# Gates of a linear recurrence: each head on its own 64 rows, both gates in one tile, the two heads in turn into two banks

## The chip, the core and the metric

The kernel runs on one core of one Trainium2 chip. The time is that of one execution on the device, in microseconds (us). The engines of the core are TensorE (matmuls; PE in the rows, PEld for its weight loads), VectorE (DVE), ScalarE (ACT), GpSimd (POOL) and SyncE (SP), which issues the DMAs. TensorE writes to PSUM, a memory of eight banks, from where VectorE or ScalarE fetch its results.

## The reference, cut to what matters

One layer of a hybrid recurrent decoder, on 1024 prompt tokens and 8 x 4 sample tokens (1056 columns in the kernel). A projection of x feeds a gated linear recurrence (RG-LRU) and a diagonal state-space branch (S5); their merge goes through an output projection, a layer norm, a convolutional feed-forward part (up, convolution, gelu, down) and a second layer norm. The change is in the gates of the recurrence:

```python
xh = xf.reshape(B_, L, LRU_HEADS, LRU_HEAD_DIM)          # 16 heads of 64
r = sigmoid(einsum('blhi,hij->blhj', xh, w_a).reshape(B_, L, D_LRU) + b_a)
i = sigmoid(einsum('blhi,hij->blhj', xh, w_x).reshape(B_, L, D_LRU) + b_x)
log_a = LRU_C * r * log_sigmoid(lam)
a = exp(log_a)
bterm = sqrt(max(-expm1(2 * log_a), 0)) * (i * xf)
h = scan(a, bterm)                                        # h_t = a_t h_{t-1} + b_t
```

Each head multiplies its 64 channels by a 64 x 64 matrix, once for gate r (`w_a`) and once for gate i (`w_x`).

## The kernel before

Activations lie with channels on the 128 partitions and tokens along the columns. The 1024 recurrence channels are eight groups j = 0 to 7 of 128, each a pair of heads ("head pair j"). All large products are made with three matmuls instead of one: an operand is split into a rounded part (`...h`, type fp32r, by ScalarE's copy) and the rest (`...l`, by VectorE's subtraction), and h x h, l x h and h x l add up in a bank (`mm3`, `split`).

For each j: `lru_in` makes the projection `psx` (three chunks of 352 columns, 24 matmuls each), copies it out and convolves it to `xc`; `lru_gate` and `s5_gate` make the projections `psl` and `psg` for the merge; `lru_rec` splits `xc` into `xch` and `xcl`, makes the gates, and runs the recurrence (`av`, `bv`, `th` with VectorE's scan, `gg`). The gate weights come from the host as 128 x 256: for each gate a 128 x 128 block with the two heads' matrices on the diagonal and zeros elsewhere (`layouts`, L1715 to L1719). `lru_weights` loads and splits them. For each gate and each of three chunks of 360 columns (the padded sequence has 1080), three matmuls write one bank (`psr`), and one activation of 128 x 360 on ScalarE applies bias and sigmoid into `gt`.

The state-space branch runs in four units (0 to 3). In each, `s5_consts` makes its tables (`tmc`, `CA`, `bk`, `psk`, `BA`, `pst`, `F32t`, `BT`) and `s5_batch` its work: `psv` (plain fp32, 64 columns of weights into 64 partitions of a bank, the two halves of the partitions in turn; one fp32 matmul is two records in the trace), the copy `V`, the scans `G`, and `psy` (plain fp32, full array). `z_split` splits its result. Small products (`psr`, `psk`, `pst`, `psv`, `psy`) share two banks ("aux"); the others use six ("mm").

At the start, x arrives in slices `xr` and is split into `xh`, `xl`; the first two weight tiles (`wx` into `wh`, `wl`) arrive in pieces, and `u_tile` multiplies slice by slice (`psu`). Behind the recurrence follow the merge (`psab`, with the tile `mm`), the output projection (`pso`), and the feed-forward products (`ps`, `pd`).

The order of all instructions on every engine is set before the launch. `Program.add` records each operation with its engine, an estimated duration and its dependences; `Program.schedule` replays them and takes, among the operations that are ready, the one of the smallest number. The numbers follow the code, shifted by the entries of the table `BOOST` (`boosted("rg3")` shifts all within). Each engine then runs its list strictly in order. The durations in `schedule` are the planner's own, not the chip's.

## Time and profile before

| | us |
|---|---|
| three runs, median | 1349.86 |
| three runs, lowest and highest | 1348.16, 1350.09 |
| the profiled execution, its own time | 1348.73 |
| its span, first to last instruction | 1347.0 |
| TensorE busy in the span | 1325.2 |
| VectorE busy | 1084.9 |
| ScalarE busy | 606.1 |
| GpSimd busy | 77.7 |

Matmuls are pipelined: each has a recorded duration of about two spacings of starts, so busy times of TensorE overlap, and what a matmul costs is read from when the next one starts. "Idle before" names what the engine waited for, put down to what came last. The granted clock of TensorE is 1.00 at its upper level and 0.50 at its lower one.

### The profile page before, as it was taken

The numbers are of one execution on the slowest core, as the hardware profiler recorded it, in microseconds if no ns is written. First come the engines' busy times: TensorE is split into PE (matmuls) and PEld (weight loads), VectorE is DVE, ScalarE is ACT, GpSimd is POOL, SyncE is SP. The second block draws the span as 40 slices with busy tenths as digits, with TensorE's granted clock in tenths as the row PEclk, the third lists the DMA queues.
The fourth block names the chain that finished last, engine by engine and source line by source line (L and its number), as shares of the span: only waits on it lengthen the run. The fifth ranks groups of instructions, "written<-read, shape, count | busy, mean of one in ns | idle before, by whom it ended". The sixth has DMA issues, their size and how long they took to land.

```text
span 1347.0 us, 24659 instructions
## 1 busy us (share of the span) xinstructions
PE 1325.2 (98%) x10044; PEld 1316.4 (98%) x10044; DVE 1084.9 (81%) x1823; ACT 606.1 (45%) x802; POOL 77.7 (6%) x184
## 2 busy tenths in 40 slices
PE   8999999999999999999999999999999999999996
PEld 8999999999999999999999999999999999999996
DVE  6996868697979986879998878878878884555797
ACT  6335545558678433355333333333332453433463
POOL 0000101110301100000100000000000000000000
PEclk9999999999999999999999999999999999999998
DMA  7524141437878770042343323232222497855251
GB/s 277 137 62 105 56 113 64 120 122 231 295 245 297 275 253 33 33 142 93 107 153 115 105 107 105 96 112 89 102 89 89 142 361 286 304 181 164 66 207 65
DMA packets 89330, 201.88 MB, mean 150 GB/s; under 512 B 11008, under 2 KB 40960, under 8 KB 89216
## 3 DMA queue, kind: packets, MB, share of 16 engines
q1 hardware_dynamic: 89216, 200.30, 44.4%
q8 instruction: 79, 1.29, 0.4%
q14 instruction: 35, 0.29, 0.1%
HBM read 142.17 MB, written 58.09 MB: 149 GB/s over the span
## 4 chain that ended last, share of the span: by engine, by line
PE 88%; DVE 7%; ACT 1%; DMA 1%; issue 1%; SPq 0%; DVEq 0%; ACTq 0%
PE ps L397 37%; PE pd L397 18%; PE pso L397 7%; PE psab L397 7%; PE psg L397 6%; PE psx L397 4%; PE psl L397 4%; PE psr L397 2%; PE psu L397 1%; PE psy L397 1%; DVE tmp L329 1%; DVE xc L341 1%; DVE tmc L329 1%; DVE wl L329 1%; DVE zl L329 1%
## 5 line engine op out<-in xcount | busy, mean ns | idle before, releaser
L397 PE MATMUL pd<-fh,dh 128*128 128x264 f32 x672 | 192.3, 286 | 0.0
L397 PE MATMUL pd<-fh,dl 128*128 128x264 f32 x672 | 191.0, 284 | 0.0
L397 PE MATMUL pd<-fl,dh 128*128 128x264 f32 x672 | 191.0, 284 | 0.0
L397 PEld LDWEIGHTS pd<-fh,dh 128*128 128x128 f32 x672 | 126.5, 188 | 0.2
L397 PEld LDWEIGHTS pd<-fl,dh 128*128 128x128 f32 x672 | 126.3, 188 | 0.2
L397 PEld LDWEIGHTS pd<-fh,dl 128*128 128x128 f32 x672 | 126.5, 188 | 0.0
L329 DVE TENSOR_TENSOR dl<-dx,dh 128x1024 fp32r<-128x1024 f32 x48 | 58.2, 1220 | 46.8 <-ACT dh L366 46.8
L397 PE MATMUL pso<-mm,wh 128*128 128x264 f32 x512 | 95.5, 287 | 0.0
L366 ACT CAST dh<-dx 128x1024 fp32r<-128x1024 f32 x48 | 49.2, 1048 | 83.3 <-PE pd L397 74.6
L341 DVE SCALAR_TENSOR_TENSOR ac<-fx,con,ac 128x1072 f32<-128x1072 f32 x48 | 64.0, 1334 | 28.0 <-ACT ac L362 27.4
L366 ACT CAST wsh<-wa 128x1024 fp32r<-128x1024 f32 x24 | 25.3, 1052 | 135.1 <-DVE wa L329 126.6
L397 PEld LDWEIGHTS pso<-mm,wh 128*128 128x128 f32 x512 | 79.8, 188 | 0.5
L397 PE MATMUL pso<-mm,wl 128*128 128x264 f32 x256 | 72.7, 284 | 0.0
L329 DVE TENSOR_TENSOR wl<-wx,wh 128x1024 fp32r<-128x1024 f32 (+2 forms) x48 | 54.1, 1130 | 18.4 <-PE psx L397 8.0
L362 ACT ACT_TABLE_LOAD x52 | 66.7, 1283 | 2.0 <-PE psy L397 1.1
L366 ACT CAST wh<-wx 128x1024 fp32r<-128x1024 f32 (+2 forms) x48 | 47.0, 982 | 39.3 <-DMA wx<-wall 19.3
L397 PE MATMUL psab<-zh,wh 128*128 128x352 f32 (+1 forms) x200 | 63.6, 318 | 0.0
L397 PE MATMUL psab<-zl,wh 128*128 128x352 f32 (+1 forms) x200 | 63.6, 318 | 0.0
L397 PE MATMUL psab<-zh,wl 128*128 128x352 f32 (+1 forms) x200 | 63.4, 317 | 0.0
L366 ACT CAST fh<-fr 128x1056 fp32r<-128x1056 f32 x42 | 44.6, 1074 | 41.0 <-PE pd L397 25.7
L397 PE MATMUL psg<-xh,wh 128*128 128x352 f32 x192 | 62.6, 326 | 0.0
L397 PE MATMUL psl<-xh,wh 128*128 128x352 f32 x192 | 62.6, 326 | 0.0
(346 smaller groups left out, 4593.9 us busy)
## 6 DMA issues: line engine op xcount, KB each, us to landing
f<-gt SPq DMA_DIRECT2D x84, 264.0 KB, 2.1
wx<-wall SPq DMA_DIRECT2D x42, 512.0 KB, 4.6
fr<-f SPq DMA_DIRECT2D x30, 528.0 KB, 4.8
wa<-wall SPq DMA_DIRECT2D x29, 512.0 KB, 4.4
wg<-wall SPq DMA_DIRECT2D x24, 512.0 KB, 3.6
dx<-wall SPq DMA_DIRECT2D x24, 512.0 KB, 4.6
dx<-s SPq DMA_DIRECT2D x24, 512.0 KB, 5.8
fr<-f SPq DMA_DIRECT2D x24, 264.0 KB, 3.6
```

What stands on the lines that cost most here:

```text
L329: pr.add("DVE", 69 + 1.0417 * fsize(out), lambda: V.tensor_tensor(out=out, in0=a, in1=b, op=op), [a, b], [out])
L341: lambda: V.scalar_tensor_tensor(out=out, in0=a, scalar=sc, in1=b, op0=op0, op1=op1),
L362: pr.add("ACT", c, lambda: S.activation(out=out, in_=a, func=f, bias=bias, scale=scale), [a] + [x for x in (bias, scale) if isap(x)], [out ...
L366: pr.add("ACT", (51 if psum(a) else 93) + 0.8333 * fsize(out), lambda: S.copy(out, a), [a], [out])
L397: T.matmul(o, lhsT=l, rhs=r, start=st, stop=sp, skip_group_check=skip)
```

## The change

The gate weights become one 128 x 128 tile per head pair: the rows of a head hold its two 64 x 64 matrices side by side, for the second head in swapped order. `lru_rec` issues, per chunk of columns, six matmuls of 64 rows x 128 columns of weights on 360 columns: the three of the first head (rows 0 to 63) into one aux bank and the three of the second (rows 64 to 127) into the other, in turn. Each bank then holds both gates of one head. Four activations of 64 partitions take them out, two per bank; one of the two writes to the other half of the partitions than it reads, and `bx` is rolled by 64 on the host for it. The planner's estimate for such a group is `share` and `more` in `mms`. The table `BOOST` is replaced as a whole (a line of each stands below), so that every list of instructions is another one.

```diff
 BOOST = {
-    "b0": -10, "b1": 1493, "b2": 1614, "b3": 1297, "c0": 190, "c1": -1072, "c2": 199, "c3": 2328, "cb1": 225,
...
+    "b1": 820, "b2": -87, "b3": 393, "c2": -694, "c3": 168, "cb0": -165, "cb1": 153, "cb2": 474, "cb3": -4263,
...
-    def mms(calls, skip=False):
+    def mms(calls, skip=False, share=1.0, more=0.0):
...
-        pr.add("PE", cost, fn, rd, wr, lat=100.0)
+        pr.add("PE", cost * share + more, fn, rd, wr, lat=100.0)
...
         def lru_weights(j):
             with boosted(f"wg{j}"):
-                wgx = mid([2, P], name=f"wgx{j}")
-                dma(wgx[:, :, :], ins["wgate"][j])
-                wgh, wgl = mid([2, P], F32R, name=f"wgh{j}"), mid([2, P], F32R, name=f"wgl{j}")
-                split(wgx[:, :, :], wgh[:, :, :], wgl[:, :, :])
+                wgx = mid([P], name=f"wgx{j}")
+                dma(wgx[:, :], ins["wgate"][j])
+                wgh, wgl = mid([P], F32R, name=f"wgh{j}"), mid([P], F32R, name=f"wgl{j}")
+                split(wgx[:, :], wgh[:, :], wgl[:, :])
...
-                for q, bn in ((0, "ba"), (1, "bx")):
-                    gt = slot([LL], name=f"gt{j}_{q}")
-                    for c in range(NCH):
-                        n = slice(360 * c, 360 * c + 360)
-                        psg = aux([360], f"psr{j}_{q}_{c}")
-                        mms(mm3(psg[:, :], wgh[:, q, :], wgl[:, q, :], xch[:, n], xcl[:, n], True, True))
-                        with boosted("e"), boosted("erec"):
-                            act(gt[:, n], psg[:, :], AF.Sigmoid, bias=cv(bn)[:, j:j + 1])
-                    gate.append(gt)
+                gate = [slot([LL], name=f"gt{j}_{q}") for q in range(2)]
+                hf = slice(0, 64), slice(64, P)
+                for c in range(NCH):
+                    n = slice(360 * c, 360 * c + 360)
+                    pa = [aux([360], f"psr{j}_{c}_{hd}") for hd in range(2)]
+                    m = [mm3(pa[hd][:, :], wgh[hf[hd], :], wgl[hf[hd], :], xch[hf[hd], n], xcl[hf[hd], n], True, True)
+                         for hd in range(2)]
+                    mms([x for y in zip(*m) for x in y], share=0.53, more=210.0)
+                    with boosted("e"), boosted("erec"):
+                        for hd in range(2):
+                            s, o = hf[hd], hf[1 - hd]
+                            act(gate[0][s, n], pa[hd][s, :], AF.Sigmoid, bias=cv("ba")[s, j:j + 1])
+                            act(gate[1][s, n], pa[hd][o, :], AF.Sigmoid, bias=cv("bx")[o, j:j + 1])
...
-    wgate = np.zeros((NK, 2, 64, 2, 2, 64), np.float32)
+    wgate = np.zeros((NK, 2, 64, 2, 64), np.float32)
...
-            wgate[:, hd, :, q, hd, :] = a[:, hd]
+            wgate[:, hd, :, q ^ hd, :] = a[:, hd]
```

Three places in the lists of instructions. A row names the line of the code, the operation, the tile that it writes and those that it reads (with a running number of the buffer) and its shape. First TensorE at the gates of head pair 0, first chunk, before (`psr_0_0` is gate and chunk):

```order
L397 MATMUL psg_2_204<-xh_101,wl_192 128x352
L397 MATMUL psr_0_0_248<-xch_245,wgh_182 128x360
L397 MATMUL psr_0_0_248<-xcl_246,wgh_182 128x360
L397 MATMUL psr_0_0_248<-xch_245,wgl_183 128x360
L397 MATMUL psr_0_1_249<-xch_245,wgh_182 128x360
L397 MATMUL psr_0_1_249<-xcl_246,wgh_182 128x360
L397 MATMUL psr_0_1_249<-xch_245,wgl_183 128x360
L397 MATMUL psx_0_261<-xh_80,wh_199 128x352
```

The same place after (`psr_0_1` is chunk and head):

```order
L397 MATMUL psg_2_204<-xh_101,wl_192 128x352
L397 MATMUL psr_0_0_249<-xch_245,wgh_182 128x360
L397 MATMUL psr_0_1_250<-xch_245,wgh_182 128x360
L397 MATMUL psr_0_0_249<-xcl_246,wgh_182 128x360
L397 MATMUL psr_0_1_250<-xcl_246,wgh_182 128x360
L397 MATMUL psr_0_0_249<-xch_245,wgl_183 128x360
L397 MATMUL psr_0_1_250<-xch_245,wgl_183 128x360
L397 MATMUL psx_0_261<-xh_80,wh_199 128x352
```

Six matmuls stay six, and the bank changes with every one instead of every third; 24 groups of six stand in the list after, and between any two of them stand twelve or more matmuls of other tiles. In unit 3 of the state-space branch, the list before has `psv` for three of its four groups in a row; after, two, then 24 `psl` matmuls, then two.

Second, VectorE up to `xcl_512`, the split for the gates of head pair 5, before (`th_473` is the scan of head pair 4, `xc_534` the convolution of head pair 7):

```order
L354 SCALAR_TENSOR_TENSOR th_473<-av_471,bv_472 128x1080
L329 TENSOR_TENSOR gg_401<-gg_401,th_473 128x1024
L329 TENSOR_TENSOR zl_507<-z_505,zh_506 128x8x128
L329 TENSOR_TENSOR zl_507<-z_505,zh_506 128x4x8
L329 TENSOR_TENSOR gg_401<-gg_401,th_473 128x32
L329 TENSOR_TENSOR wl_567<-wx_565,wh_566 128x1024
L329 TENSOR_TENSOR spv_1201<-spv_1201,spz_1200 128x1024
L341 SCALAR_TENSOR_TENSOR xc_534<-xp_533,con,xc_534 128x1080
L329 TENSOR_TENSOR zl_510<-z_508,zh_509 128x8x128
L341 SCALAR_TENSOR_TENSOR xc_534<-xp_533,con,xc_534 128x1080
L329 TENSOR_TENSOR zl_510<-z_508,zh_509 128x4x8
L329 TENSOR_TENSOR xcl_512<-xc_446,xch_511 128x1080
```

The same place after:

```order
L329 TENSOR_TENSOR spv_1201<-spv_1201,spz_1200 128x1024
L329 TENSOR_TENSOR bv_472<-bv_472,gt_1_464 128x1080
L329 TENSOR_TENSOR zl_507<-z_505,zh_506 128x8x128
L329 TENSOR_TENSOR zl_507<-z_505,zh_506 128x4x8
L329 TENSOR_TENSOR av_471<-av_471,th_473 128x1080
L329 TENSOR_TENSOR wl_567<-wx_565,wh_566 128x1024
L329 TENSOR_TENSOR zl_510<-z_508,zh_509 128x8x128
L329 TENSOR_TENSOR zl_510<-z_508,zh_509 128x4x8
L348 MEMSET av_471 128x8
L341 SCALAR_TENSOR_TENSOR xc_534<-xp_533,con,xc_534 128x1080
L329 TENSOR_TENSOR xcl_512<-xc_446,xch_511 128x1080
L354 SCALAR_TENSOR_TENSOR th_473<-av_471,bv_472 128x1080
```

The scan, both products with it and one of the steps of `xc_534` now stand behind `xcl_512`; otherwise the same work stands ahead of it.

Third, SyncE's DMAs at the very start, before (`wx_73` and `wx_76` are the first two weight tiles, `xr` the slices of x, `con` the constants):

```order
L376 DMA wx_73<-wall 128x256
L376 DMA xr_79<-xT 128x352 x3
L376 DMA xr_82<-xT 128x352 x3
L376 DMA wx_73<-wall 128x256
L376 DMA wx_76<-wall 128x256
L376 DMA xr_85<-xT 128x1056
L376 DMA xr_88<-xT 128x1056
```

The same place after:

```order
L376 DMA wx_73<-wall 128x512
L376 DMA wx_73<-wall 128x256
L376 DMA xr_79<-xT 128x352 x3
L376 DMA xr_82<-xT 128x352 x3
L376 DMA con<-con 128x964
L376 DMA wx_76<-wall 128x256 x2
L376 DMA wgx_181<-wgate 128x128
L376 DMA xr_85<-xT 128x1056
```

The last 512 columns of the first weight tile moved to the front, and the constants and a gate tile ahead of the third slice of x (`xr_85`). On TensorE, `psu` follows the slices in turn in both.

## Rows read from the trace of the kernel before

**Rows 1.** The page, engines: busy us (share of the span) and instructions.

```profile
PE 1325.2 (98%) x10044; PEld 1316.4 (98%) x10044; DVE 1084.9 (81%) x1823; ACT 606.1 (45%) x802; POOL 77.7 (6%) x184
```

**Rows 2.** Waits of TensorE: us in total, times, longest us.

```profile
PE psu L397 <- ACT xh L366: 4.3, 1, 4.3
PE psr L397 <- DVE xcl L329: 2.4, 1, 2.4
PE psv L397 <- ACT V L366: 1.1, 1, 1.1
PE psk L397 <- DVE bk L345: 1.1, 1, 1.1
PE pst L401 <- DVE F32t L329: 0.6, 1, 0.6
...
```

**Rows 3.** Tile `psr`: duration min/median/max in ns, first and last start, form.

```profile
L397 PEld LDWEIGHTS psr<-xch,wgh x48: 186/188/330, 125.7 to 429.7; 128*128 128x128 f32 x48
L397 PE MATMUL psr<-xch,wgh x48: 322/327/502, 125.9 to 429.8; 128*128 128x360 f32 x48
...
L362 ACT ACTIVATE gt<-psr,con x48: 550/561/573, 126.6 to 432.4; 128x360 f32<-128x360 f32 x48
```

**Rows 4.** Tile `psv`, its weight loads, columns as in rows 3.

```profile
L397 PEld LDWEIGHTS psv<-U,BT x128: 132/137/138, 81.5 to 283.7; 128*64 128x64 f32 x128
```

**Rows 5.** Timeline of TensorE at a group of gates: start us, us, instruction.

```profile
125.87 0.33 PE L397 MATMUL psr<-xch,wgh 128*128 128x360 f32 x1
...
126.87 0.32 PE L397 MATMUL psx<-xh,wh 128*128 128x352 f32 x1
```

**Rows 6.** Timeline of TensorE around `psv` and behind `psy`.

```profile
140.24 0.32 PE L397 MATMUL psx<-xh,wl 128*128 128x352 f32 x1
140.49 1.15 PE L397 MATMUL psv<-U,BT 128*64 128x136 f32 x16
141.57 0.43 PE L397 MATMUL psl<-xh,wh 128*128 128x352 f32 x1
141.84 0.32 PE L397 MATMUL psl<-xl,wh 128*128 128x352 f32 x1
...
283.43 0.68 PE L397 MATMUL psv<-U,BT 128*64 128x136 f32 x8
...
306.12 0.42 PE L397 MATMUL psx<-xh,wh 128*128 128x352 f32 x1
```

**Rows 7.** Chain that ended last, a piece with `psy`: start us, us, what.

```profile
303.59 2.78 PE psy L397 x24
```

**Rows 8.** Timeline of TensorE at the gates of head pair 5.

```profile
374.77 0.33 PE L397 MATMUL psr<-xch,wgh 128*128 128x360 f32 x1
377.50 0.67 PE L397 MATMUL psr<-xcl,wgh 128*128 128x360 f32 x1 [2.40 <-DVE xcl L329]
...
380.63 0.34 PE L397 MATMUL psg<-xh,wl 128*128 128x352 f32 x1
```

**Rows 9.** Windows: us, busy us of PE, PEld, DVE, ACT, POOL; PEclk, DMA share, GB/s.

```profile
377.20:380.60 3.40, 3.10 (x10) 3.10 (x11) 3.40 (x4) 2.15 (x5) 0.00 (x0) 0.50 0.56 183
...
404.00:438.00 34.00, 34.00 (x212) 34.00 (x211) 33.84 (x39) 28.85 (x38) 5.76 (x4) 1.00 0.85 296
```

**Rows 10.** Timeline of VectorE ahead of that `xcl`.

```profile
363.11 2.41 DVE L354 TENSOR_TENSOR_SCAN th<-av,bv 128x1080 f32<-128x1080 f32 x1
365.55 1.23 DVE L329 TENSOR_TENSOR gg<-gg,th 128x1024 f32<-128x1024 f32 x1
...
374.78 1.34 DVE L341 SCALAR_TENSOR_TENSOR xc<-xp,con,xc 128x1080 f32<-128x1080 f32 x1
...
376.16 1.28 DVE L329 TENSOR_TENSOR xcl<-xc,xch 128x1080 fp32r<-128x1080 f32 x1
```

**Rows 11.** Timeline of TensorE, the first matmul.

```profile
4.26 0.66 PE L397 MATMUL psu<-xh,wh 128*128 128x352 f32 x1 [4.26 <-ACT xh L366]
```

**Rows 12.** DMA view of the first 40 us: GB/s in 40 slices of 1 us.

```profile
GB/s 0 13 285 279 251 278 304 295 323 285 347 370 427 420 398 422 399 392 396 398 395 409 396 393 293 220 298 103 12 0 0 82 291 152 236 292 304 211 231 386
```

More of the change, by code (lines that the diff above doesn't have):

```diff
@@ L1019, in lru_rec @@
             wgh, wgl = GW.pop(j)
-            gate = []
             with boosted(f"rg{j}"):
@@ L1697, in layouts @@
     con = np.concatenate([
-        col(i["lru_conv_w"][0].reshape(-1)), col(i["lru_conv_b"][0]), col(i["lru_ba"][0]), col(i["lru_bx"][0]),
+        col(i["lru_conv_w"][0].reshape(-1)), col(i["lru_conv_b"][0]), col(i["lru_ba"][0]), np.roll(col(i["lru_bx"][0]), 64, 0),
         col(i["lru_lambda"][0]), col(i["ln1_g"][0]), col(i["ln1_b"][0]), col(i["ln2_g"][0]), col(i["ln2_b"][0]),
@@ L1718, in layouts @@
         for hd in range(2):
-            wgate[:, hd, :, q, hd, :] = a[:, hd]
-    r = {"xT": xT, "wall": wall, "con": con, "scon": scon, "wgate": wgate.reshape(NK, P, 2, P)}
+            wgate[:, hd, :, q ^ hd, :] = a[:, hd]
+    r = {"xT": xT, "wall": wall, "con": con, "scon": scon, "wgate": wgate.reshape(NK, P, P)}
     return {k: np.ascontiguousarray(a) for k, a in r.items()}
```

68 rows, old and new, of the table BOOST are left out of this document.

## The prediction

> **What bounds the kernel now.** I read the engine line of the page first: TensorE is busy for 1325.2 of 1347.0 us, VectorE for 81%, ScalarE for 45% [rows 1]. So the change is worth what it takes from TensorE's own work, plus what it removes or adds of the moments in which TensorE stands. The second view is the list of what TensorE waited for, and it is short: 4.3 us for the first operand, 2.4 us for `xcl`, 1.1 us each for a copy of `V` and for `bk`, 0.6 us for `F32t`, and a smaller one [rows 2]. All of these lie ahead of 380 us; behind that point reordering has nothing to win.
>
> **The gates.** Before, one chunk of one gate is three matmuls of 128 rows on 360 columns, and there are 144 of them [rows 3]. They are pipelined, so their recorded 0.33 us is no price; the spacing of starts is. Six of them start at 125.87 us and the next other matmul at 126.87 us [rows 5]: 1.00 us for six, 0.166 us each, and 24 x 1.00 = 24.0 us in all.
>
> After, the count stays at 144, but each reads 64 rows, and two in a row use different halves of the array and different banks. If a pair runs together, a chunk costs three spacings instead of six. No instruction of before uses half of the rows, but `psv` uses half of the columns, in the same alternation, and is the nearest row. Sixteen `psv` take 1.15 us and eight take 0.68 us [rows 6]: eight more cost 0.47 us, 0.059 us each. `psy`, of the same 136 columns and type on the full array, takes 2.78 us for 24, 0.116 us each [rows 7]. So two halves do run together there, at the price of one.
>
> The same stretch prices the change of shape. From the last full matmul ahead of the sixteen (start 140.24 us) to the second one behind them (141.84 us) pass 1.60 us [rows 6]. Two full spacings of 0.16 and eight pairs of 0.116 make 1.25 us; 0.35 us are lost, in a gap ahead of the first `psv` and in a slow first matmul behind (0.43 us). A 64-column load took 0.137 us [rows 4] and a 128-column one 0.188 us [rows 3], and the new groups load 128 columns, so I add 0.05: 0.40 us per group. The order shows 24 groups with full-array work between all of them, so all 24 pay.
>
> A group after: 3 x 0.165 + 0.40 = 0.895 us against 1.00. **24 x 0.105 = 2.5 us gained.** The bounds: a switch that costs nothing would give 12.1 us; halves that don't run together would cost 24 x 0.40 = 9.6 us. I take 2.5, since `psv` is the one row with a partial array and both its parts are measured there.
>
> The Trainium skill, page "TensorE: Matmul & The Clock Gate", section "LDWEIGHTS (loading the stationary operand)", says that a load takes as long as its columns make it, whatever the number of rows: 107 ns for 128 columns. If the two loads of a pair also followed each other, a pair would take 0.213 us by this figure, and the gates would cost an estimated 0.9 us more than before. The page "TensorEngine Tiling (Array Packing)", section "Tiling Modes", says on the other side that different tiles load and multiply in parallel; `psv` agrees with that one for halves of the columns, and no run here shows it for halves of the rows.
>
> **The eviction.** A chunk of both gates was emptied by two activations of 128 x 360, 0.56 us each [rows 3]; now it is four of 64 x 360. Half the partitions leave the columns as they were, so I price each at the same 0.56: 48 more, 27 us on an engine that is 45% busy. Both auxiliary banks stay taken for some 2.2 us instead of 1.1, and most groups have 24 matmuls of 0.16 us (3.9 us) between them, which covers it. Between the second and third chunk of head pair 6 there are only twelve (1.9 us): I add **0.4 us** for that. The gate weights halve; their DMAs and splits lie on queues and engines with room, priced at zero.
>
> **The stall at 374.8 us.** The first matmul of the gates of head pair 5 starts at 374.77 us, the second at 377.50, because `xcl` came late [rows 8]; the granted clock is 0.50 from 377.2 to 380.6 us, the lower of its two levels, after TensorE had stood for 2.40 us [rows 8, 9]. The price: 2.73 - 0.17 = 2.56 us of standing, then 3.13 us for the ten matmuls from 377.50 to 380.63 us, which take 1.63 us at the upper level, so 1.50 more. Together 4.1 us. VectorE was busy all the way ahead of that `xcl`. In its new order the scan (2.41), its product (1.23) and one step of the next convolution (1.34) stand behind `xcl` instead of ahead of it [rows 10]: 5.0 us, twice what the standing needs. What is late next there is the last split of `z`, which still precedes `xcl`, and ScalarE's `xch`. **I take the whole 4.1 us as gained**; the other bound is zero.
>
> **The `V` wait.** In unit 3 of the state-space branch three groups of `psv` stood in a row on two banks, and the third waited 1.1 us for ScalarE [rows 2]. Now two stand in a row, then 24 full matmuls, then two, as in units 1 and 2, for which no such wait is listed. **1.1 us gained.**
>
> **The start.** The new DMA order puts 256 KB of the first weight tile ahead of everything, and the 482 KB of constants ahead of the second tile's weights. At the 280 GB/s of the first microseconds [rows 12] the first matmul, at 4.26 us before [rows 11], comes 0.9 us later, and the third slice of x, with 802 KB more ahead of it, 2.9 us later. TensorE's first pass needs these slices in turn, so it falls 2.9 us behind. Part is absorbed: the waits for `bk` and `F32t`, 1.7 us [rows 2], are set by VectorE's chain of parameters, whose inputs have the same bytes ahead of them as before. I take 2.9 - 1.7 = **1.2 us lost**; the bounds are 0 and 2.9.
>
> **The rest of the order.** From 404 to 438 us VectorE is busy for 33.84 of 34.00 us beside a full TensorE [rows 9]. An earlier TensorE finds the same backlog there. I price it at zero, because nothing on TensorE waited there, and keep it as a rival.
>
> **The sum.** -2.5 - 4.1 - 1.1 + 1.2 + 0.4 = -6.1 us. The profiled execution took 1348.73 us, so 1342.6; the median of the three runs is 1.1 us above that execution, so I forecast 1343.8 us (rounded from 1343.7).
>
> **The rivals.**
> 1. *The halves don't run together*, since halves of the rows differ from halves of the columns: both write all 128 partitions, though to two banks. For it: no row of before shows it done. Against it: `psv`. The term of -2.5 becomes +9.6: 1355.9 us, slower. It decides from the point at which a pair takes over 0.25 us: a group then costs 1.15 us, and 24 x 0.15 eats the 3.6 us that the other terms give.
> 2. *The loads of a pair follow each other.* By the load rows, 64 more columns take 0.051 us longer, so 128 columns stream in 0.102 us; a pair then takes 0.204 us, a group 1.01, in all 2.8 us more than forecast: 1346.6 us. `psv` doesn't exclude it: two loads of 64 columns would need 0.102 us, and a pair there takes 0.118.
> 3. *The switch is cheaper*, because part of the 0.35 us behind `psv` belongs to a change of type (the first matmul behind `psy`, with no change of shape, is slow too, 0.42 us [rows 6]), and the gates have the type of their neighbours. At 0.20 us per group 4.8 us less: 1339.0 us.
> 4. *The stall stays or moves* to another late operand of VectorE: 1347.9 us.
> 5. *VectorE or ScalarE takes it back* from 404 us on: VectorE is full there, and ScalarE's 28.85 of 34 us [rows 9] grow by twelve activations, 6.7 us, to over 35. TensorE then waits for banks or for its operands until most of the 6.1 us is gone: 1348.8 us.
>
> **How the numbers follow.** The forecast gets 0.42, rival 1 0.07, rival 2 0.08, rival 3 0.15, rival 4 0.13, rival 5 0.10, and 0.05 are left for waits at places that I did not follow. The time is the forecast's. The range takes in rival 3 and a little below it, and reaches up past rivals 4 and 5; it leaves out rival 1 and the cheapest switch: 1337 to 1350.5 us. A measurement can tell about 0.2%, 2.7 us, so faster means below 1347.2 us. The forecast and rival 3 lie there, most of rival 2 and a third of rivals 4 and 5: 0.74. Within 0.2% lie the rest of those: 0.17. Slower: rival 1 and part of the unknown, 0.09.
>
> **What would show it.** In the profile after: starts of a `psr` pair some 0.01 us apart and pairs 0.165 us apart (0.20 for rival 2, equal steps of 0.165 for rival 1); 0.90 + 0.32 us from the last full matmul ahead of a group to the second behind it; no wait of TensorE for `xcl` and `V`, and no second stretch at the lower clock; the first matmul near 5.2 us and a shorter wait for `bk`. I am wrong on the order if TensorE waits for VectorE or ScalarE anew, above all behind 404 us.

## The result, and the profile after

The changed kernel is slower: a median of 1357.9 us (four runs, 1355.9 to 1358.5) against 1349.0 us for the kernel before on the same chip, a ratio of 1.0064 with an interval of 1.0047 to 1.0082. The forecast was 1343.8 us and a range that ended at 1350.5. The profiled execution took 1357.9 us, with a span of 1356.1.

The engine line of the page of after, to set beside [rows 1]:

```profile
PE 1325.7 (98%) x10044; PEld 1305.4 (96%) x10044; DVE 1084.2 (80%) x1823; ACT 626.5 (46%) x845; POOL 87.9 (6%) x184
```

It tells little: TensorE is busy for as long as before in a span that is 9 us longer, so it stands for 30.4 us instead of 21.8. Where, the line doesn't say. ScalarE has 20 us more. The waits of TensorE of after (us in total, times, longest), beside [rows 2], tell more:

```profile
PE psr L397 <- ACT gt L362: 5.6, 1, 5.6
PE psu L397 <- ACT xh L366: 5.4, 1, 5.4
PE psg L397 <- ACT xp L366: 3.5, 1, 3.5
PE pst L401 <- DVE BA L329: 1.5, 1, 1.5
PE psy L397 <- POOL H L369: 1.2, 2, 1.0
PE psk L397 <- DVE bk L345: 1.0, 1, 1.0
...
```

The two waits that the prediction wanted gone, `xcl` and `V`, are gone. Two longer ones stand in their place, 5.6 and 3.5 us, on operands that it did not name, and the first operand comes 1.1 us later.

Tile `psr` of after (duration min/median/max in ns, first and last start), beside [rows 3], and TensorE's timeline at a group of gates, beside [rows 5]:

```profile
L362 ACT ACTIVATE gt<-psr,con x96: 540/557/562, 129.3 to 444.2; 64x360 f32<-64x360 f32 x96
L397 PEld LDWEIGHTS psr<-xch,wgh x48: 182/183/283, 128.5 to 441.7; 64*128 64x128 f32 x48
...
```

```profile
...
128.29 0.32 PE L397 MATMUL psg<-xh,wl 128*128 128x352 f32 x1
128.55 0.43 PE L397 MATMUL psr<-xch,wgh 64*128 64x360 f32 x2
128.82 0.33 PE L397 MATMUL psr<-xcl,wgh 64*128 64x360 f32 x2
128.99 0.32 PE L397 MATMUL psr<-xch,wgl 64*128 64x360 f32 x2
129.24 0.43 PE L397 MATMUL psx<-xh,wh 128*128 128x352 f32 x1
129.51 0.33 PE L397 MATMUL psx<-xl,wh 128*128 128x352 f32 x1
```

Each line "x2" is a pair; its two starts lie 3 ns apart, and so do the starts of its two loads. From the last full matmul ahead to the second behind pass 129.51 - 128.29 = 1.22 us (1.214 by the unrounded starts), of which 0.32 are the full ones: 0.894 us for a group.

**Where the time went.** Start of the same matmul in both traces, us:

| matmul | before | after | lag |
|---|---|---|---|
| first `psu` | 4.26 | 5.38 | +1.12 |
| last `psu` | 53.35 | 55.76 | +2.41 |
| last `psl` of head pair 0 | 81.25 | 84.56 | +3.31 |
| first `psk` of unit 3 | 247.52 | 251.16 | +3.63 |
| last `psl` of head pair 5 | 283.18 | 284.80 | +1.62 |
| last `psl` of head pair 7 | 363.03 | 364.45 | +1.41 |
| first `psab` | 393.39 | 403.98 | +10.60 |
| first `pso` | 492.49 | 502.42 | +9.93 |
| first `plsq`, near the end | 1333.66 | 1342.90 | +9.24 |

At the last `psl` of head pair 5 the lists differ: after, two groups of `psv` are still to come there, before only one. Behind the last `psv` the lag is 2.08 us.

Nearly all of the loss falls between 364 and 404 us, behind which a little is gained back. TensorE's timeline there has two holes:

```profile
364.45 0.32 PE L397 MATMUL psl<-xh,wl 128*128 128x352 f32 x1
368.24 0.43 PE L397 MATMUL psg<-xh,wh 128*128 128x352 f32 x1 [3.47 <-ACT xp L366]
...
386.23 0.32 PE L397 MATMUL psg<-xh,wl 128*128 128x352 f32 x1
392.12 1.24 PE L397 MATMUL psr<-xch,wgh 64*128 64x360 f32 x2 [5.57 <-ACT gt L362]
```

3.79 and 5.89 us from start to start, and behind each the granted clock falls, as in [rows 9]. Windows of after (busy us of PE, PEld, DVE, ACT, POOL; PEclk, DMA share, GB/s):

```profile
364.40:368.30 3.90, 0.43 (x4) 0.14 (x2) 3.59 (x4) 2.64 (x5) 0.54 (x2) 1.00 0.82 196
368.30:373.10 4.80, 4.80 (x20) 4.80 (x21) 4.80 (x4) 2.81 (x5) 4.75 (x4) 0.64 1.03 419
386.20:392.10 5.90, 0.35 (x3) 0.06 (x1) 5.87 (x7) 0.57 (x2) 5.27 (x2) 0.84 0.45 181
392.10:397.00 4.90, 4.88 (x17) 4.19 (x18) 0.45 (x1) 4.80 (x9) 0.00 (x0) 0.50 0.28 110
```

The 20 matmuls of the second window take 3.2 us at the upper level, so 1.6 are lost; the last window's 4.9 us would be some 2.5 us, by the group at 128.55 and ten spacings of 0.16. The two holes cost 3.6 + 1.6 and 5.7 + 2.4, together 13.3 us; the stall on `xcl` (4.1 us) is saved against it. 13.3 - 4.1 = 9.2, which is the step from +1.41 to +10.60.

What filled the holes stands on ScalarE and GpSimd (timelines of after):

```profile
363.38 2.21 ACT L366 CAST zh<-z 128x1024 fp32r<-128x1024 f32 x2
...
367.74 1.23 ACT L366 COPY xp<-psx 128x352 f32<-128x352 f32 x4 [1.26 <-DVE zl L329]
...
391.51 1.14 ACT L362 ACTIVATE gt<-psr,con 64x360 f32<-64x360 f32 x2 [6.09 <-POOL states L369]
```

```profile
384.22 7.25 POOL L369 COPY states<-th 128x1 f32<-128x1 f32 x2 [10.94 <-DVE th L354]
```

*First hole.* `xp` empties the banks of `psx` for the next product. It stands behind casts of `z` in ScalarE's list, and then waits another 1.26 us for VectorE's `zl`: `xp` and `z` take their buffers from the same pool (`temp`), and `zl` is the last reader of a `z`. *Second hole.* The second gate's tile takes the slot (a buffer of a pool that many tiles share) of an older `th`, two of whose last readers are copies on GpSimd of 128x1 and 128x8. They start behind the scan of `th`, which the new order puts behind `xcl`, and take 7.25 us. ScalarE waits for the slot, both auxiliary banks stay full, and TensorE waits for a bank. Before, the second gate's tile was wanted three chunks later.

### The profile page after: what moved, and what is told of

Its sections match the earlier page's. It is cut to its first block, busy times and chain, and to the rows that moved or that the text cites. A ratio compares the mean times of both kernels' runs of the same rounds, so it can differ in the third digit from the quotient of the medians.

```text
span 1356.1 us, 24760 instructions
## 1 busy us (share of the span) xinstructions
PE 1325.7 (98%) x10044; PEld 1305.4 (96%) x10044; DVE 1084.2 (80%) x1823; ACT 626.5 (46%) x845; POOL 87.9 (6%) x184
## 4 chain that ended last, share of the span: by engine, by line
PE 87%; DVE 7%; ACT 3%; issue 1%; DMA 1%; POOL 1%; SPq 0%; DVEq 0%; ACTq 0%; POOLq 0%
PE ps L397 36%; PE pd L397 18%; PE psab L397 7%; PE pso L397 7%; PE psg L397 5%; PE psx L397 5%; PE psl L397 4%; PE psr L397 1%; PE psu L397 1%; PE psy L397 1%; DMA xr<-xT 1%; DVE tmp L329 1%; DVE xc L341 1%; DVE tm L329 1%; ACT gt L362 1%
## 5 line engine op out<-in xcount | busy, mean ns | idle before, releaser
L397 PE MATMUL psg<-xl,wh 128*128 128x352 f32 x192 | 63.1, 329 | 0.0
L397 PE MATMUL psx<-xh,wh 128*128 128x352 f32 x192 | 63.1, 329 | 0.0
L397 PE MATMUL psg<-xh,wl 128*128 128x352 f32 x192 | 63.1, 328 | 0.0
```

The lines of the kernel that those rows point to most:

```text
L397: T.matmul(o, lhsT=l, rhs=r, start=st, stop=sp, skip_group_check=skip)
```

## The experiments

Ratios are against the kernel before on the same chip, with their 95% interval.

**1. The table and the gates apart.** Two kernels cross the parts of the change: the new gates with the old table, the old gates with the new table. The same table doesn't give the same lists, since the planner replays other operations with it.

```diff
 BOOST = {
-    "b1": 820, "b2": -87, "b3": 393, "c2": -694, "c3": 168, "cb0": -165, "cb1": 153, "cb2": 474, "cb3": -4263,
+    "b0": -10, "b1": 1493, "b2": 1614, "b3": 1297, "c0": 190, "c1": -1072, "c2": 199, "c3": 2328, "cb1": 225,
...
```

That is the first line of new_gates_old_table, made from the changed kernel; old_gates_new_table is the kernel before with the same exchange the other way round.

> The gates of the changed kernel with the table of numbers of the kernel before, everything computed. Theory 1 (the moved order costs, the gates themselves save): the 24 groups of gates save 2.5 us as their gaps show, the two new stalls (364 and 386 us) and the later start are gone, the old stall of 375 us on `xcl` is back; 1349.0 - 2.5 = 1346.5 us, ratio 0.998. Theory 2 (the gates' new form makes the stall at 386 us: both gate tiles are wanted at the first chunk, and four evictions instead of two empty the banks): a wait of `psr` on ScalarE's `gt` of 3 to 6 us, with 2 to 3.5 us of lower clock behind it, is there in this order too, in some head pair; 1352 to 1356 us, ratio 1.002 to 1.005.

Measured: 1381.5 us, 1.0243 (1.0222 to 1.0264). Both theories were far too low. Its waits:

```profile
PE psg L397 <- ACT xp L366: 17.2, 1, 17.2
PE psl L397 <- ACT gs L362: 7.7, 1, 7.7
...
PE psr L397 <- ACT gt L362: 3.9, 4, 1.2
```

Two groups of one head pair stand in a row there, at 344 us, and show in the open what a group costs its banks:

```profile
344.46 0.43 PE L397 MATMUL psr<-xch,wgh 64*128 64x360 f32 x2
...
346.43 0.43 PE L397 MATMUL psr<-xch,wgh 64*128 64x360 f32 x1 [1.21 <-ACT gt L362]
347.57 0.43 PE L397 MATMUL psr<-xch,wgh 64*128 64x360 f32 x1 [0.71 <-ACT gt L362]
```

Four evictions of 0.56 us empty two banks in 2.2 us, while the matmuls of a group take 0.9.

> The gates of the kernel before with the table of numbers of the changed kernel, everything computed. Theory 1 (the order alone brings the stalls): both stalls stay, and the gates give back the 2.5 us that they saved: 1357.9 + 2.5 = 1360.4 us, ratio 1.008. Theory 2 (the stall at 386 us needs the new form): the first gate's three chunks go through before the second gate's tile is wanted, the stall at 386 us (5.9 us standing, some 3.4 us of lower clock) is gone and the one at 364 us (3.8 and 1.7 us) stays: 1360.4 - 9.3 = 1351 us, ratio 1.0015.

Measured: 1352.8 us, 1.0034 (1.0021 to 1.0047), between the two expectations and nearer the second. The wait at 386 us falls from 5.6 to 2.2 us, and the one at 364 us from 3.5 to 0.7, which neither theory had said:

```profile
...
PE psab L397 <- ACT sb L362: 2.5, 1, 2.5
PE psr L397 <- ACT gt L362: 2.2, 1, 2.2
...
PE psg L397 <- ACT xp L366: 0.7, 1, 0.7
```

The 2.2 us are another wait than the 5.6. In ScalarE's list here the cast of a weight tile stands ahead of `gt`, and ScalarE waits 4.31 us for that tile's DMA, until 388.03 us; the slot of the second gate's tile is not what is missing, and so far theory 2 was right. GpSimd's copies of `th` take 15.0 us in this kernel (from 369.59 us), and nothing is seen to wait for them.

So with the old gates the new table costs some 4.6 us, and the new gates come on top: some 33 us with the old table, 4 to 5 us with the new one, although they save 2.5 us on TensorE. My first theory ("the gates save, the order costs") falls. How much of this is the gates' form stays open, since the lists are other ones too: with the new table and the old gates the scan of `th` stands ahead of `xcl` again (367.13 and 374.15 us), with the new gates behind it. That six more evictions for each head pair, 3.3 us more on ScalarE ahead of everything behind them in its list, make both holes deeper, is argued from the rows and not shown alone.

**2. The slot of the second gate.**

```diff
+def vgcopy(out, a):
+    pr.add("POOL", 600 + 1.0 * fsize(out), lambda: V.tensor_copy(out=out, in_=a), [a], [out])
...
-gcopy(olru[:, j, 27:28], h[:, 1023:1024])
+vgcopy(olru[:, j, 27:28], h[:, 1023:1024])
...
-gcopy(olru[:, j, 28:36], hq[:, :, 3])
+vgcopy(olru[:, j, 28:36], hq[:, :, 3])
```

The planner goes on placing them as GpSimd's, so that the order of everything else stays; VectorE makes them.

> The changed kernel with the two small copies of `th` into the states (128x1 and 128x8), which GpSimd made in 7.25 us, made on VectorE; everything computed. Theory 1 (TensorE stood 5.9 us at 386 us because those two copies held the slot of the second gate's tile): the slot comes free some 7 us earlier, the stall of 5.9 us and the 3.4 us lost at lower clock behind it are gone, 1357.9 - 9.3 = 1348.6 us, ratio 0.9997 against the kernel before. Rival (ScalarE is late there anyway, since the scan that fills `th` was moved behind `xcl`): VectorE's scan ends at 384.2 us, but the copies stand further down VectorE's list and the eviction comes as late; 1356 to 1358 us, ratio 1.005 to 1.0065.

Measured: 1352.1 us, 1.0027 (1.0016 to 1.0037), 5 to 6 us below the changed kernel. The wait on `gt` is down to 0.8 us; ScalarE's eviction comes at 387.59 us and not at 391.51. Theory 1 had the place and the mechanism right. It put the gain at 9.3 us: it took the clock at 3.4 us where the window above has 2.4, it had nothing left of the standing where 0.9 us stay, and the first hole grew by 1.0 us in this execution.

```profile
...
PE psg L400 <- ACT xp L366: 4.5, 1, 4.5
...
PE psr L400 <- ACT gt L362: 0.8, 1, 0.8
```

**3. The heads not in turn.**

```diff
-mms([x for y in zip(*m) for x in y], share=0.53, more=210.0)
+mms([x for y in m for x in y], share=0.53, more=210.0)
```

> The changed kernel with the six matmuls of a group as three of the first head, then three of the second, and not in turn; everything computed. Theory 1 (two matmuls on 64 rows each run side by side only when they stand next to each other in the list): six in a row take 6 x 0.165 + 0.40 = 1.39 us and not 0.895, or 1.22 us where the third and the fourth still pair up: 24 x 0.33 to 24 x 0.50 = +8 to +12 us, 1366 to 1370 us, ratio 1.0125 to 1.0155. Rival (TensorE runs ahead in its list and pairs them whatever their order): no change, 1357.9 us, ratio 1.0064.

Measured: 1357.4 us, 1.0068 (1.0049 to 1.0086): no change. Theory 1 is refuted. In TensorE's timeline of this kernel the pairs stand as before, although the list has three of the first head, then three of the second:

```profile
128.08 0.44 PE L397 MATMUL psr<-xch,wgh 64*128 64x360 f32 x2
128.35 0.34 PE L397 MATMUL psr<-xcl,wgh 64*128 64x360 f32 x2
128.52 0.33 PE L397 MATMUL psr<-xch,wgl 64*128 64x360 f32 x2
```

The two starts of a pair lie 10 ns apart instead of 3. The turn-taking in the change is worth nothing; the halves are. And the statement ahead of the prediction that each engine runs its list strictly in order does not hold for TensorE here: the fourth matmul of a group started before the second and third.

**4. The length of the casts of `z`.** Both holes lie behind operations on `z`. The planner takes a cast of 1024 columns for 93 + 0.8333 x 1024 = 946 ns, whatever its pattern. The trace of after has 2.2 us on ScalarE for it, and as much on VectorE for the remainder, against 1.05 us for a weight tile:

```profile
L366 ACT CAST wh<-wx 128x1024 fp32r<-128x1024 f32 x42 | 44.0, 1050 | 28.3 <-DMA wx<-wall 20.8 <-DVE wl L329 6.0 <-PE psab L397 1.3
L366 ACT CAST zh<-z 128x1024 fp32r<-128x1024 f32 x4 | 8.9, 2222 | 0.0
```

The columns here are line, engine, operation, tiles and form, then busy us and mean ns. The experiment writes `zh` and `zl` in plain order. It leaves out the order of the columns that the reference wants in the product behind them, so the three kernels with it show what the long casts cost and are no cure. The lists of all engines stay as they were.

```diff
-return (x[:, :SEQ].rearrange("p (n j) -> p j n", j=8),
+return (x[:, :SEQ].rearrange("p (j n) -> p j n", j=8),
```

> The changed kernel, in which the casts of the four `z` tiles and their remainders (`zh`, `zl`) write their 1024 columns in the order in which they are read, not eight columns apart, so that the columns of the gated product come out in another order than the reference wants them (that part of the result is not the reference's; the number and size of all instructions and their order are unchanged). In the changed kernel a cast of `z` took 2.22 us on ScalarE and its remainder 2.17 us on VectorE, against 1.05 and 1.22 us for the 1024 columns of a weight tile. Theory 1 (the stall at 364 us stands since ScalarE and VectorE have eight such operations in their lists ahead of the copies `xp` that empty the banks): two casts and two remainders stand ahead of `xp`, each shorter by about 1.0 us, so that the stall of 3.8 us falls to 1 to 2 us and the 1.7 us of lower clock behind it go: 1357.5 - 4 = 1353.5 us. Rival (the arrival of `z` by DMA or the banks themselves set it): the stall stays above 3 us; 1357 us.

Measured: 1346.6 us, 0.9978 (0.9969 to 0.9987): 11 us less than the changed kernel, nearly three times what theory 1 expected. The casts take 1.04 us, and both holes are nearly shut:

```profile
L366 ACT CAST zh<-z 128x1024 fp32r<-128x1024 f32 x4 | 4.2, 1041 | 2.7 <-DMA z<-zs 2.7
```

```profile
...
PE psg L397 <- ACT xp L366: 1.2, 1, 1.2
...
PE psr L397 <- ACT gt L362: 0.7, 2, 0.5
```

The second hole shuts too, without a touch on the copies of `th`: VectorE reaches the scan 4.6 us earlier (GpSimd's copies start at 379.62 us, not 384.22, and take 2.24).

> Both edits in the changed kernel: the two small copies of `th` on VectorE, and `zh`, `zl` written in the order in which they are read (that part of the result is not the reference's). Theory 1: both stalls of the changed kernel are gone or small, 1352.1 (with the copies alone) - 4 to - 5 = 1347 to 1348 us; what is left against the 1348.1 us of the kernel before is the start (+1.9 to +2.4 us), the waits of `psk` and `pst` (+0.9) and `psy` (+1.1) against the gates (-2.5) and `psv` (-1.8). Rival (the stall moves on to the next late operand of ScalarE once more): 1351 to 1352 us.

Measured: 1346.8 us, 0.9982 (0.9973 to 0.9992), close to theory 1. The two edits don't add, since either shuts the second hole.

> The kernel before, with `zh` and `zl` written in the order in which they are read (that part of the result is not the reference's): what the same edit gives there. Theory 1 (the long casts of `z` are also what made `xcl` late at 375 us in the kernel before): the stall of 2.56 us and the 1.5 us of lower clock behind it go, 1348.1 - 4.1 = 1344 us. Rival (it hangs on the place of `xcl` in VectorE's list, not on the length of what stands ahead): 1347.5 to 1348.5 us.

Measured: 1345.5 us, 0.9976 (0.9966 to 0.9985). The wait on `xcl` is gone from the list of the kernel before as well, so the long casts were its cause too; the prediction had it as a matter of the order alone. With short casts the old gates are 1.1 us ahead of the new ones by the medians, in the given orders. The intervals against the kernel before overlap, but all nine runs of plain_z_before (up to 1346.0 us) lie below all ten of plain_z on the same chip (from 1346.2). So of the 8.9 us that the change costs, all but some 1.1 are gone when the casts are short.

**5. The start.** Entries of the table, put side by side:

```diff
-"ws00": 555, "ws02": -1943, "ws04": 747, "ws12": -102, "ws14": -2497,
+"ws00": 3029, "ws02": 363, "ws04": -277, "ws10": 850, "ws12": 243,
...
-"xs0": 99, "xs1": -26, "xs2": -1564, "xs3": -2236,
+"xs0": 1852, "xs1": 672, "xs2": 354, "xs3": 1237,
...
```

> The changed kernel, with the numbers of the start alone (the weights of the first product and the slices of the input) taken from the table before; everything computed. Theory 1 (the loads' new order at the start costs 2.4 us that nothing behind takes back): the first matmul starts at 4.3 us and not 5.4 us, and the 2.4 us of lag at the end of the first product fall to 0.5 us or less; 1357.5 - 1.9 to - 2.4 = 1355 to 1355.6 us. Rival (the waits of `psk`, `pst` and `psy` behind the start are set by VectorE and GpSimd, which gain nothing): they grow by what the start gives back, 1357 us.

Measured: 1357.2 us, 1.0063 (1.0046 to 1.0080); the 1.6 us at stake are too few to be told from the changed kernel. In the trace the start behaves as theory 1 says: first matmul at 4.27 us, a lag of 0.79 us at the end of `psu` instead of 2.41, and nothing taken back by `psk` and `pst`. At the second hole 1.1 us of the gain are left (a lag of 9.51 at `psab` against 10.60).

**6. Three attempts at short casts with the right result.** First, read with a jump and write neighbours:

```diff
-return (x[:, :SEQ].rearrange("p (n j) -> p j n", j=8),
+return (x[:, :SEQ].rearrange("p (n j) -> p n j", j=8),
...
-src = (z[:, :, 8:136], z[:, 0:4, 0:8])
+src = (z[:, :, 8:136].rearrange("p j n -> p n j"), z[:, 0:4, 0:8].rearrange("p q b -> p b q"))
```

> The changed kernel, in which the casts of `z` and their remainders walk through the tile in the order of the result: they write `zh` and `zl` column by column and read `z` 136 columns apart, where they read it column by column and wrote eight columns apart; everything computed, instructions and order unchanged. Theory 1 (it is the strided writing that makes such a cast take 2.22 us instead of 1.05): 1.05 to 1.3 us for a cast, the stalls at 364 and 386 us as small as with the plain order, 1346 to 1348 us, faster than the kernel before by 0 to 0.2%. Rival (a stride of either side costs the same): 2.2 us for a cast, both stalls stay, 1357 us.

> The same edit in the kernel before, everything computed. Theory 1 (the writing costs): as with the plain order, the stall on `xcl` at 375 us goes, 1345 to 1346 us, and the old gates stay 1 us ahead of the new ones, since both kernels have lost what their lists waited for and the new order keeps its later start and its waits of `psk`, `pst` and `psy`. Rival (either side costs): 2.2 us for a cast, 1348 us.

Measured: 1355.6 us, 1.0041 (1.0020 to 1.0061), and 1347.1 us, 0.9992 (0.9980 to 1.0004). The rival holds: the casts take 2.20 and 2.27 us. A jump costs the same on either side. The changed kernel scattered here from 1351.5 to 1358.1 us. In the one execution profiled (1355.8 us) the copies of `th` took 4.73 us, and the wait at the second hole was 3.1 us instead of 5.6; in that of heads_not_in_turn (1355.6 us) they took 4.73 us and the wait was 2.1. So the depth of the second hole varies between executions, which fits the scatter; one profile can't show that it is all of it.

Second, let TensorE make the jump:

```diff
+v = x[:, :NT].rearrange("p (j n) -> p j n", j=8)
+return [v[:, :, 0:128]] + [v[:, 4 * i:4 * i + 4, 128:132] for i in range(2)]
...
+def zc(x, n):
+    return x[:, :NT].rearrange("p (j n) -> p n j", j=8)[:, n.start // 8:n.stop // 8, :]
...
-hi[:, q, k, :], lo[:, q, k, :], Z[k][0][:, n], Z[k][1][:, n], k == 0, k == 3)])
+hi[:, q, k, :], lo[:, q, k, :], zc(Z[k][0], n), zc(Z[k][1], n), k == 0, k == 3)])
```

> The changed kernel with `zh` and `zl` written as eight runs of 128 columns (as they are read, and the last 32 columns beside them), and the product behind them (`psab`) reads its moving operand 132 columns apart instead, so that the result is the reference's; everything computed. Theory 1 (TensorE reads columns that lie apart as fast as neighbouring ones): casts of 1.05 us, `psab` at 161 ns a matmul as before, both stalls small: 1346 to 1347.5 us, ratio 0.998 to 1.000. Rival (TensorE pays for the stride as ScalarE and VectorE do): 504 matmuls of `psab` at 200 ns and more, +20 us or more, 1370 us.

> The same edit in the kernel before, everything computed. Theory 1: no stall at 375 us, 1345 to 1346 us, ratio 0.997 to 0.9985, 1 us ahead of the changed kernel with the same edit, since there the start and the waits of `psk`, `pst` and `psy` eat what the gates save. Rival (TensorE pays for the stride): 1368 us or more.

Measured: 1427.7 us, 1.0576 (1.0560 to 1.0591), and 1426.8 us, 1.0569 (1.0553 to 1.0585). TensorE pays as well, 302 ns for a matmul of `psab` instead of 161; two neighbours in the list of z_by_matmul, spaced by 0.30 us:

```profile
409.71 0.48 PE L397 MATMUL psab<-zh,wl 128*128 128x352 f32 x1
410.01 0.48 PE L397 MATMUL psab<-zh,wh 128*128 128x352 f32 x1
```

Ahead of `psab` the expectation comes true: the old gates reach it 3.75 us earlier than the kernel before, the new ones 0.53.

The same kernels with the copies of `th` on VectorE, with a table for each kind of gates that was chosen for short casts, and for the new gates with the price of a group that experiment 7 names:

> The new gates with short casts of `z`, the small copies of `th` on VectorE and a table of numbers of their own for that; everything computed. Theory 1 (without stalls the gates are worth their 2.5 us): 1345.5 (the kernel before with short casts) - 2.5 = 1343 us, and 2 to 3 us less than the old gates under an order of their own. Rival (both gate tiles wanted at once and four evictions for two banks cost in any order what the matmuls save): 1345 to 1347 us, no better than the old gates.

> The old gates with the same edits (short casts of `z`, the small copies of `th` on VectorE) and a table of numbers of their own for that; everything computed. Theory 1: no stall is left that the table could take away but those of the start and of the first S5 unit, 1344 to 1346 us, 2 to 3 us above the new gates under an order of their own. Rival: within 1 us of the new gates.

Measured: 1426.9 us, 1.0568 (1.0550 to 1.0585), and 1427.6 us, 1.0576 (1.0560 to 1.0592). Neither time reaches what was expected, for the slow `psab`; what can be compared is the pair. The new gates are 0.7 us ahead, and all their four runs lie below the other four. But the old gates' table leaves a wait of 3.2 us at `psk` for `bk`, against 1.1 there and 1.2 at `pst` for the new ones, so the pair compares two tables as much as two kinds of gates.

Third, pairs of neighbours on both sides: the casts write every second column, `psab` reads two neighbours and jumps.

```diff
-v = x[:, :NT].rearrange("p (j n) -> p j n", j=8)
+v = x[:, :NT].rearrange("p (g n h) -> p g h n", g=4, h=2)
...
-    return x[:, :NT].rearrange("p (j n) -> p n j", j=8)[:, n.start // 8:n.stop // 8, :]
+    return x[:, :NT].rearrange("p (g n h) -> p n g h", g=4, h=2)[:, n.start // 8:n.stop // 8, :, :]
```

> The kernel before, in which `zh` and `zl` hold the eight columns of a step as four pairs of neighbours: the casts write every second column and read neighbours, and `psab` reads two neighbours and then jumps; everything computed. Theory 1 (what costs is a jump at every column, not a jump at every second one): casts of 1.05 to 1.2 us, `psab` at 161 ns a matmul, no wait for `xcl` at 375 us: 1345.5 us as with the plain order, ratio 0.997 to 0.9985. Rival (any pattern that is not plain costs): casts of 2.2 us or `psab` above 200 ns, 1348 us or more than 1368 us.

> The new gates with the same layout of `zh` and `zl`, the small copies of `th` on VectorE, and a table of numbers of their own; everything computed. Theory 1 (without stalls the gates are worth their 2.5 us): 1345.5 - 2.5 = 1343 us, 2 to 3 us below short_casts_old_gates. Theory 2 (two gate tiles and four evictions at once cost as much in any order): 1345 to 1347 us, no better than the old gates. Rival on the layout: as there, above 1368 us if `psab` pays.

Measured: 1429.3 us, 1.0606 (1.0591 to 1.0620), and 1428.5 us, 1.0597 (1.0583 to 1.0612). Theory 1 is right for ScalarE and wrong for TensorE (short_casts_old_gates):

```profile
L366 ACT CAST zh<-z 128x1024 fp32r<-128x1024 f32 x4 | 4.6, 1154 | 4.2 <-DMA z<-zs 4.2
```

1.15 us for a cast, but a spacing of 306 ns for `psab`. The new gates are 0.8 us ahead, but under an order of their own against the given one.

**7. Orders that allow for the long casts.** Everything as in the kernels given, except the copies of `th` on VectorE, the group's measured price in the planner (the change's 0.53 x 985 + 210 = 732 ns is below the 894 measured; new gates only), and a table for each kind of gates that was chosen with 2.2 us for a cast of `z`.

```diff
-mms([x for y in zip(*m) for x in y], share=0.53, more=210.0)
+mms([x for y in zip(*m) for x in y], share=0.53, more=370.0)
...
-gcopy(olru[:, j, 27:28], h[:, 1023:1024])
+vcopy(olru[:, j, 27:28], h[:, 1023:1024])
...
```

> The new gates with the casts of `z` as in the changed kernel, the small copies of `th` on VectorE, and a table of numbers that was made for casts of `z` of 2.2 us; everything computed. Theory 1 (the loss lay in the order, the gates themselves gain 2.5 us): no stall above 2 us is left between 360 and 395 us, 1346 to 1348 us, 0 to 0.2% below the kernel before, and below the old gates under such an order. Theory 2 (two gate tiles and four evictions at once, with two banks, cost in every order what the matmuls save): stalls of 1 to 3 us on `xcl`, `xp` or `gt` stay in that stretch, 1348 to 1352 us, 2 to 4 us above the old gates under such an order.

> The old gates with the casts of `z` as they are, the small copies of `th` on VectorE, and a table of numbers that was made for casts of `z` of 2.2 us; everything computed. Theory 1: the stall on `xcl` goes (2.56 us and 1.5 us of lower clock), 1344 to 1346 us, within 1 us of the new gates or above them. Theory 2: 1344 to 1346 us, ratio 0.997 to 0.9985, and 2 to 4 us below the new gates.

Measured: 1351.6 us, 1.0022 (1.0013 to 1.0031), and 1344.4 us, 0.9966 (0.9953 to 0.9978). **The old gates under such an order are the fastest kernel here that computes everything**, faster than both kernels given. Its waits are few:

```profile
PE psu L402 <- ACT xh L371: 4.3, 1, 4.3
PE pst L406 <- DVE BA L334: 1.2, 1, 1.2
PE psv L402 <- ACT V L371: 1.0, 1, 1.0
```

For the new gates the waits beside the gates stayed, in another place again (new_gates_long_casts):

```profile
PE psr L404 <- ACT gt L369: 2.3, 2, 1.6
PE psk L404 <- DVE bk L352: 2.2, 1, 2.2
PE psg L404 <- ACT gg L369: 1.9, 1, 1.9
...
PE psg L404 <- ACT xp L373: 1.1, 1, 1.1
```

The times are those of theory 2, but only part of the 7.3 us between the two is the gates'. At the last `psl` of head pair 2 this kernel is 3.7 us later than the kernel before (4.7 us of lateness come ahead of its first gate, from the start and the first S5 unit of the table found for it), the old gates' one 0.5 us earlier. From there to the end the new gates gain 1.2 us on the kernel before, the old ones 3.7: in that stretch, which holds all but the first head pair's gates, the new ones are 2.5 us worse. That holds for these two tables, of which each is only the best that was found.

## Why the prediction was wrong

**The gates (-2.5): right.** 0.894 us for a group against 0.895 forecast, pairs 3 ns apart, loads in parallel. That the 0.40 us for the change of shape fits so closely is in part luck: it was carried over from another type and from halves of the columns. Rivals 1, 2 and 3 are false. The Trainium skill, page "TensorEngine Tiling (Array Packing)", section "Tiling Modes", was the one to follow.

**The eviction (+0.4): the step that failed, with the right price.** "48 more, 27 us on an engine that is 45% busy", and "most groups have 24 matmuls of 0.16 us (3.9 us) between them, which covers it". An eviction of half the partitions does take the same 0.56 us, and there are 48 more. But cover was sought on TensorE's side alone, and every new wait of the change was put at these 0.4 us; the two holes measure 13.3. Cover is no help in either. In the first, TensorE waits for `xp`, behind the gates' work and the casts of `z` in ScalarE's list, which the evictions lengthen by 3.3 us a head pair. In the second it is the next group of gates that waits, with 24 matmuls between, because ScalarE's eviction itself stood for 6.09 us for the slot of the second gate's tile. Nor is there room to catch up there, whatever the shares over the span. From 355 to 400 us, with short casts, VectorE (third) and ScalarE (fourth) were busy like this with the new gates and order (plain_z), then with the old ones (plain_z_before):

```profile
355.00:400.00 45.00, 43.17 (x268) 40.78 (x267) 41.05 (x42) 37.82 (x54) 6.16 (x7) 1.00 0.81 291
```

```profile
355.00:400.00 45.00, 45.00 (x282) 45.00 (x281) 35.38 (x37) 30.96 (x45) 7.21 (x7) 1.00 0.81 279
```

The change thus puts 5.7 us more work on VectorE and 6.9 us more on ScalarE into these 45 us. By an estimate from their lengths, the long casts add 3.8 us on VectorE (44.9 of 45) and 4.7 us on ScalarE (42.5 of 45). plain_z shows that the long casts are needed for both holes; how the rest divides between the evictions and the new lists is not shown. And the prediction did not see that the new form wants both gate tiles, hence two slots, at the first chunk and not the second one three chunks later; th_copies_on_vector shows what that wait cost, 5 to 6 us.

**The stall on `xcl` (-4.1): gone, and come back threefold.** "What is late next there is the last split of `z`, ... and ScalarE's `xch`" looked as far as `xcl` and not at what hung on the operations that had moved. The scan that was moved behind `xcl` to free it is what GpSimd's copies of `th` wait for. Rival 4, "the stall stays or moves", was right in kind, at 13.3 us instead of 4.1, with ScalarE's operands and not VectorE's at the end of the chain. The cause that holds for the old stall and for both new ones, casts of `z` at twice the length that the order allows for, stood in the trace of before (2.3 us each on ScalarE and on VectorE) and was not read: the prediction took `z`'s splits as fixed.

**The `V` wait (-1.1): right.** No wait for `V` is left, and from the first `psv` of unit 3 to the `psg` behind its last the lag falls from 3.38 to 2.08 us, by 1.3.

**The start (+1.2): mis-sized.** The gross lag was 2.4 us instead of 2.9, but the waits that were to absorb 1.7 us of it absorbed none: `bk` came as much later as its reader, with 1.05 us of waiting as before. Only at 111 us, at `psk` of unit 1, TensorE takes 0.7 us back, where two short waits for `CA` are gone. start_labels_of_before, with the loads' old order, has the lag at 0.79 us.

**What was missing:** 0.9 us at `pst` and 1.1 us at `psy`, which now wait for `BA` and `H`.

**The sum by measured terms:** -2.5 (gates) - 4.1 (`xcl`) - 1.3 (`psv`) + 2.4 (start) - 0.7 (`psk`) + 2.0 (`pst`, `psy`) + 13.3 (two holes) = +9.1; the last lag is +9.24. Rival 5, a loss behind 404 us, is false: the lag shrinks there from 10.6 to 9.2 us.

**What the gates are worth.** Without the long casts the new gates come out between 1.1 us behind the old ones (given orders) and 0.7 us ahead (an order for each, beside a slow `psab`); with the long casts they are behind in every order tried. So the 2.5 us that they save on TensorE never showed in full; that they are spent on banks, slots and ScalarE is what the waits suggest. Whether a better order would keep more of them stays open, as does a cure for the long casts with the right result: none of the three patterns tried was free.

## What to carry to other kernels

A saving on the busiest engine can be paid for on the engines that empty its banks: count how many instructions a change adds there, and price them in the stretch where that engine is fullest, in its own list, not by its share of the span. Before trusting an order made by a planner, compare its price of each operation with the trace, form by form; here four casts and their remainders at twice their price were behind the old stall and both new ones. A wait removed by moving an operation is only removed if everything that hung on the moved operation, on every engine, still comes in time.

## What the runs showed of the hardware

**A small copy on GpSimd mostly ends when an instruction of VectorE ends.** The same two copies of `th` (128x1 and 128x8) took 0.32 us in all at 445.87 us, 0.66 at 230.56, 1.71 at 156.74, 2.24 at 351.88 and 7.25 at 384.22 in one trace, and 4.73 at the place of the 7.25 in two other kernels:

```profile
445.87 0.32 POOL L369 COPY states<-th 128x1 f32<-128x1 f32 x2 [4.79 <-DVE th L354]
```

VectorE was busy all through these windows, but for 0.04 us. Taken one by one, a copy mostly ends within 0.06 us of the end of an instruction that VectorE ran beside it (90 of 96 copies of `th` in six traces). The 128x1 copy at 351.88 us lasts to 352.98, VectorE's `spy` to 352.93; the 128x8 copy behind it lasts to 354.12, VectorE's `wl` to 354.07. The short scans at 230.56 hold the copies in the same way (0.32 and 0.34 us each), and so does a `TENSOR_SCALAR` in the trace of before (copy to 345.17, VectorE to 345.12). Beside a product that reads PSUM (445.87) the copies took 0.19 us each and didn't wait for its end. At 384.22 the first copy let six such ends pass (7.12 us, then 0.19 for the second), and in old_gates_new_table one took 14.28 us; why is not shown. The Trainium skill, page "SBUF — State Buffer", section "Who interferes with whom", says that a VectorE instruction with two inputs in SBUF contends with a GpSimd instruction that reads SBUF; these rows agree for such instructions. On VectorE the two copies took 0.15 us each.

**A jump at every column about doubles ScalarE's and VectorE's time, on the write side (8 columns) and on the read side (136) alike** (2.2 against 1.05 us, and 2.15 to 2.17 against 1.22); writing every second column costs 0.1 us on ScalarE and nothing on VectorE (1.22). TensorE pays 302 ns instead of 161 for columns 132 apart, and 306 for pairs of neighbours. The Trainium skill, page "SBUF — State Buffer", section "Door 1: The DMA port swizzle", in the note on cachelines, asks for two hits in each line of 16 bytes at full bandwidth: the casts agree, TensorE's pairs do not.

**TensorE pairs matmuls on different halves of the rows whatever their order in the list.** Three of one half followed by three of the other ran as three pairs, 10 ns apart (heads_not_in_turn).
